# Making a row tile's scale on GpSimd instead of VectorE in a cumulative-difference matmul

## The chip, the core and the metric

One core of a Trainium2 chip runs the whole kernel. Its engines are TensorE (PE in the profile; its weight loads are PEld), VectorE (DVE), ScalarE (ACT), GpSimd (POOL) and SyncE (SP), which issues the DMAs. The metric is the device time of one execution in microseconds (us). The kernel before took 1449.84 us, the median of 3 runs (1449.72 to 1450.08).

## The reference

```python
def reference(x, w):                      # x: 8 x 2048 x 2048, w: 2048 x 2048, float32
    cs = np.cumsum(x, axis=1)
    diff = cs - np.concatenate([np.zeros(...), cs[:, :-1, :]], axis=1)
    return np.matmul(diff, w).astype(np.float32)
```

The difference of the cumulative sums is x itself up to rounding, so what is to be computed is x @ w: a 16384 x 2048 matrix times a 2048 x 2048 matrix.

## The kernel before

**Tiles.** x is cut into 128 row tiles of 128 rows. The first four (rows 0 to 3 in the code's counting of tiles) are multiplied in bf16 in a plain way while the weights are still being loaded. The other 124, tiles 4 to 127, go in groups of four through a Strassen-like scheme of fewer products on float16 blocks of W (`B11` to `B22`, and their differences `T1` to `T4`), with sums of row tiles made on VectorE. Products collect in PSUM; ACT copies them out with a scale (`keep`, line 636), VectorE adds further ones (`add`, line 639), and stores go out on SP's queue.

**Scales.** Row tiles and weights are brought into the range of float16 first. For W, ACT sums up absolute values (`measure`, line 273), VectorE takes the maximum (`greatest_of_w`, line 288), GpSimd makes an all-reduce over the partitions out of it (line 289), once for each half of W's columns, and VectorE makes the reciprocal (`scale_of_w`, lines 293 and 294), with which W's blocks are scaled (`block`, lines 342 and 346).

For each of the 124 row tiles the steps are:

1. `load` (line 113): two DMAs on SP's queue bring the 128 x 2048 tile into one of a few places in `F`.
2. `weigh` (line 125): ACT sums the absolute values of each half into a column of the small tile `of`; two operations of 128 x 1024.
3. `scale_of` (lines 142 and 144): VectorE adds the two sums, with a floor (`m`), and takes the reciprocal (`s`), both 128 x 1.
4. `unit_of` (line 150): GpSimd multiplies `uw`, the scale of W's two halves, by `m`. The result is the factor of `keep` and `add`.
5. `narrow` (line 164): ACT writes the tile in float16, multiplied by `s`; two operations.
6. `turn` (line 177): two transposing DMAs on SP's queue bring the float16 tile into the layout of TensorE's stationary operand (`x`).

**Order.** Each engine works through its own queue in order. The helper `after` chains the operations of one engine in the order in which the program asks for them. The start-up (lines 184 to 514), a first group (`group_plain`) and a second one (`group_half`) are written out by hand; all further groups follow the list `ORDER`, in which each step has its place (`scale.h`, `unit.h`, `narrow0.h` and so on). In the start-up the scale of tile 4 is asked for while the right half of W is still being brought in, before its maximum is known; the units and the scales of tiles 6 and 5 come behind that maximum. The first group uses tiles 4, 6, 5 and 7 in this order: its third product reads tile 6, its fifth a sum made out of tile 5.

**GpSimd's queue before.** Besides four memsets it holds a change of its configuration (MODIFY_POOL_CONFIG), the two all-reduces, another change of configuration, and the 124 operations of `unit_of`.

Of the kernel before, what the change touches and what calls it, by code (L numbers as in the profile page):

```python
# [10 lines left out]
def kernel(  # L11
# [6 lines left out]
    nc = tc.nc  # L18
    P = 128
# [10 lines left out]
    f32 = mybir.dt.float32  # L30
    ADD = mybir.AluOpType.add
    SUB = mybir.AluOpType.subtract
    MUL = mybir.AluOpType.mult
    MAX = mybir.AluOpType.max
# [5 lines left out]
    TINY = 1e-34  # L40
# [11 lines left out]
    const = ctx.enter_context(tc.tile_pool(name="const", bufs=1))  # L52
# [19 lines left out]
    uw = const.tile([P, 2], f32, name="uw")  # L72
    uinv = const.tile([P, 2], f32, name="uinv")

    waste = const.tile([P, NH], mybir.dt.uint8, name="waste")
    F = const.tile([P, 5, NH], f32, name="F")
    turned_x = [
# [10 lines left out]
    def after(engine, ask):  # L88
        if engine in last:
            with tc.issue_after(last[engine].ins):  # L90
                said = ask()
        else:
            said = ask()
        last[engine] = said[-1] if isinstance(said, tuple) else said
        return said
# [38 lines left out]
    def scale_of(t):  # L134
        if t < END:
            m2 = sums_of.pop(t)
            m, s = (m2[:, i : i + 1] for i in (2, 3))
            u = m2[:, 4:6]
            scales[t], unit[t] = s, u
            after(  # L140
                "dve",
                lambda: nc.vector.tensor_scalar(m, m2[:, :1], m2[:, 1:2], TINY, ADD, MAX),  # L142
            )
            after("dve", lambda: nc.vector.reciprocal(s, m))  # L144
            sizes[t] = m

    def unit_of(t):
# [38 lines left out]
    with ExitStack() as head:  # L186
# [229 lines left out]
        def bring(ko):  # L416
            fetch(1, ko)
            cast(1, ko)
            measure(1, ko)
            if ko == AHEAD:  # L420
                scale_of_w(0)
            if ko > AHEAD:
                turn_left(1)
            if ko == 10:
                load(PLAIN, 0)
                load(PLAIN, 1)
                weigh(PLAIN)
                scale_of(PLAIN)
            if ko == 11:
                narrow(PLAIN)  # L430
# [51 lines left out]
        for k in range(KH):  # L482
            block(B12, 0, 1, k, "dve")
            if k == 1:
                scale_of(PLAIN + 2)
            if k % 2:
                if k // 2:
                    finish_row(k // 2)
# [12 lines left out]
        turn(PLAIN + 2)  # L501
        weigh(PLAIN + 1)
        scale_of(PLAIN + 1)
        unit_of(PLAIN + 1)
        narrow(PLAIN + 1)
# [830 lines left out]
```

## Time and profile before

| what | value |
|---|---|
| time, median of 3 runs | 1449.84 us |
| span of the profiled execution, first to last instruction | 1447.4 us |
| TensorE busy | 1437.9 us (99%) |
| VectorE busy | 1319.0 us (91%) |
| ACT busy | 970.5 us (67%) |
| GpSimd busy | 43.8 us (3%) |
| TensorE in the chain that ended last | 97% |

The profile gives the span of the one profiled execution and no separate time for it beyond that; the runs are timed apart from it. A row of the timeline begins with the start in us from the span's start and the busy time in us, then the engine, the line, the operation, output and inputs, shapes, and how many operations the row merges; the idle time of the engine just before it and the event that seems to have ended it stand in brackets. A row of the view by line gives lowest, median and highest duration in ns, then the first and the last start in us. A row of the table by stretches gives the stretch, its length, and the busy times of PE, PEld, DVE, ACT and POOL, the granted TensorE clock, the DMA share and GB/s. POOLq is GpSimd's queue, SPq that of SyncE.

### The profile page before, as it was taken

To read this page: it belongs to the slowest core of one execution; us is meant where nothing else is said; L and a number is where in the kernel's file an instruction comes from. 1 tells how busy PE (TensorE), PEld (TensorE's weight loads), DVE (VectorE), ACT (ScalarE), POOL (GpSimd) and SP (SyncE) were. 2 spreads that over 40 slices of the span, in tenths; PEclk is the share of its full clock that TensorE was granted. 3 is DMA by queue.
4 is the path that set the end of the run, shared out by engine and by line. 5 is a ranking of instruction groups with operands and counts; after the bars stand their busy time and mean duration, and the time that the engine had idled before them with its cause. 6 is when DMAs were issued, how large, how long until landed. Compare 5 with 4: busy or idle time off the path is not lost.

```text
span 1447.4 us, 20191 instructions
## 1 busy us (share of the span) xinstructions
PE 1437.9 (99%) x6686; PEld 651.6 (45%) x6692; DVE 1319.0 (91%) x2310; ACT 970.5 (67%) x1472; POOL 43.8 (3%) x130
## 2 busy tenths in 40 slices
PE   8999999999999999999999999999999999999998
PEld 4444444444444444444444444444444444444443
DVE  4899899999999999999999999999999999999998
ACT  6987566666666776666666667666667766666662
POOL 0011000000000000000000000000000000000000
PEclk9999999999999999999999999999999999999999
DMA  9999788899888898888899888998878998889973
GB/s 363 368 257 298 200 234 232 239 253 253 226 224 239 238 254 245 231 233 236 248 247 232 234 238 233 262 240 234 228 234 240 252 234 239 226 242 248 255 200 127
DMA packets 378199, 351.58 MB, mean 243 GB/s; under 512 B 274800, under 2 KB 274800, under 8 KB 377968
## 3 DMA queue, kind: packets, MB, share of 16 engines
q1 hardware_dynamic: 378096, 350.31, 86.5%
q8 instruction: 52, 0.85, 0.2%
q14 instruction: 51, 0.42, 0.1%
HBM read 150.99 MB, written 134.22 MB: 197 GB/s over the span
## 4 chain that ended last, share of the span: by engine, by line
PE 97%; DMA 2%; DVE 0%; SPq 0%; issue 0%; DVEq 0%
PE b L628 62%; PE b L609 33%; PE b L304 2%; DMA W<-in_w_dram 2%; DMA W<-in_x_dram 0%; DVE c L639 0%; PE b L464 0%; SPq L225 0%; DVE wb L267 0%; SPq L259 0%; DVEq L267 0%; DVEq L639 0%
## 5 line engine op out<-in xcount | busy, mean ns | idle before, releaser
L639 DVE SCALAR_TENSOR_TENSOR c<-b,of,c 128x512 f32<-128x512 f32 x790 | 573.6, 746 | 71.1 <-PE b L628 61.4
L609 PE MATMUL b<-W,x 128*128 128x512 f16 x2144 | 507.1, 379 | 0.0
L636 ACT ACTIVATE c<-b,of 128x512 f32<-128x512 f32 x492 | 312.7, 680 | 220.2 <-PE b L628 113.8
L628 PE MATMUL b<-W,x 128*128 128x512 f16 x1904 | 454.9, 379 | 0.0
L164 ACT ACTIVATE F<-F,of 128x1024 f16<-128x1024 f32 x246 | 282.3, 1148 | 175.6 <-DVE of L144 173.4
L628 PEld LDWEIGHTS <-x 128*128 128x128 f16 x2500 | 244.6, 98 | 295.4 <-issue 1.0
L609 PEld LDWEIGHTS <-x 128*128 128x128 f16 x2144 | 209.7, 98 | 253.3 <-issue 0.5
L125 ACT ACTIVATE waste<-F 128x1024 uint8<-128x1024 f32 x246 | 259.3, 1054 | 8.3 <-DMA F<-in_x_dram 6.2
L628 PEld LDWEIGHTS <-inner 128*128 128x128 f16 x1644 | 160.8, 98 | 194.0
L628 PE MATMUL b<-W,inner 128*128 128x512 f16 x940 | 241.2, 379 | 0.0
L599 DVE TENSOR_TENSOR x<-x,x 128x1024 f16<-128x1024 f16 (+1 forms) x390 | 227.1, 583 | 3.3
L628 PE MATMUL b<-flow,x 128*128 128x512 f16 x584 | 149.9, 379 | 0.0
L628 PE MATMUL b<-inner 128*128 128x512 f16 x472 | 121.1, 379 | 0.0
L955 DVE TENSOR_TENSOR flow<-W 128x2048 f16<-128x2048 f16 x87 | 105.7, 1215 | 0.0
L1053 DVE TENSOR_TENSOR b<-b,c 128x512 f32<-128x512 f32 x116 | 80.4, 693 | 12.7 <-PE b L628 12.7
L150 POOL TENSOR_SCALAR of<-uw,of 128x2 f32<-128x2 f32 x124 | 42.6, 357 | 1299.6 <-DVE of L142 717.1
L955 DVE TENSOR_TENSOR flow<-W,inner 128x2048 f16<-128x2048 f16 x58 | 70.7, 1220 | 0.0
L1046 ACT COPY c<-b 128x512 f32<-128x512 f32 x58 | 33.4, 576 | 51.2 <-PE b L628 51.2
L304 PE MATMUL b<-wb,xP 128*128 128x512 bf16 x234 | 53.2, 379 | 2.2 <-ACT wb L265 1.1
L599 DVE TENSOR_TENSOR inner<-x 128x512 f16<-128x512 f16 x117 | 49.3, 421 | 3.1 <-DMA x<-F 1.0
L1046 ACT COPY b<-b 128x512 f32<-128x512 f32 x87 | 51.2, 589 | 0.2 <-PE b L628 0.2
L599 DVE TENSOR_TENSOR inner<-x,inner 128x512 f16<-128x512 f16 x117 | 49.2, 421 | 2.0
(68 smaller groups left out, 517.5 us busy)
## 6 DMA issues: line engine op xcount, KB each, us to landing
F<-in_x_dram SPq DMA_DIRECT2D x246, 512.0 KB, 5.2
out_dram<-c SPq DMA_DIRECT2D x492, 256.0 KB, 3.0
W<-in_w_dram SPq DMA_DIRECT2D x32, 512.0 KB, 8.4
W<-in_x_dram SPq DMA_DIRECT2D x16, 256.0 KB, 7.8
x<-F SPq DMA_TRANSPOSE x246, 3.4
out_dram<-o SPq DMA_DIRECT2D x5, 256.0 KB, 7.0
out_dram<-wb SPq DMA_DIRECT2D x5, 256.0 KB, 7.0
xP<-in_x_dram SPq DMA_DIRECT2D x1, 1024.0 KB, 6.4
```

Of the source, the lines that this page charges most:

```text
L125: lambda: nc.scalar.activation(waste, where[t][i], ABS, scale=1.0 / ROW, accum_out=sums_of[t][:, i : i + 1],),
L150: after("pool", lambda: nc.gpsimd.tensor_scalar(u, uw, m, None, MUL))
L164: lambda: nc.scalar.activation(narrowed(t)[:, ds(i * NH, NH)], where[t][i], COPY, scale=s),
L304: lambda: nc.tensor.matmul(ps[r][n], xP[:, r, ko, :], wb[h, ko][:, ds(n * NB, NB)], start=(ko == 0), stop=(ko == KO - 1),),
L599: after("dve", lambda: nc.vector.tensor_tensor(dst.all, p.all, q.all, op))
L609: said = nc.tensor.matmul(to[n], a[k], b[k][:, n, :], start=(first and k == 0), stop=(k == KH - 1), skip_group_check=True,)
L628: said = nc.tensor.matmul(to, a[k], b[k], start=(first and k == 0), stop=(k == 3), skip_group_check=True)
L636: after("act", lambda: nc.scalar.activation(c, p, COPY, scale=u))
L639: after("dve", lambda: nc.vector.scalar_tensor_tensor(c, p, u, c, MUL, ADD))
L955: after("dve", lambda: nc.vector.tensor_tensor(in_twos(to), x, y, op))
L1046: after("act", lambda: nc.scalar.copy(c, p))
L1053: after("dve", lambda: nc.vector.tensor_tensor(t, p, s, ADD))
```

## The change

The two small operations of `scale_of` are asked of GpSimd. The second is no reciprocal there but a power: the tensor `m` raised, element by element, to a constant tensor `minus` that holds -1, which VectorE writes once at the start of the program.

```diff
     uinv = const.tile([P, 2], f32, name="uinv")
 
+    minus = const.tile([P, 1], f32, name="minus")
+    nc.vector.memset(minus, -1.0)
     waste = const.tile([P, NH], mybir.dt.uint8, name="waste")
...
             after(
-                "dve",
-                lambda: nc.vector.tensor_scalar(m, m2[:, :1], m2[:, 1:2], TINY, ADD, MAX),
+                "pool",
+                lambda: nc.gpsimd.tensor_scalar(m, m2[:, :1], m2[:, 1:2], TINY, ADD, MAX),
             )
-            after("dve", lambda: nc.vector.reciprocal(s, m))
+            after(
+                "pool",
+                lambda: nc.gpsimd.tensor_tensor(s, m, minus, mybir.AluOpType.pow),
+            )
             sizes[t] = m
```

In the changed kernel the sum stands in line 144, the power in line 148, `unit_of` in line 155, `narrow` in line 169 and the all-reduce in line 294.

## The prediction

> **What bounds the kernel now.** I read the page first, then the busy times of stretches of the span.
>
> ```profile
> span 1447.4 us, 20191 instructions
> PE 1437.9 (99%) x6686; PEld 651.6 (45%) x6692; DVE 1319.0 (91%) x2310; ACT 970.5 (67%) x1472; POOL 43.8 (3%) x130
> ...
> PE 97%; DMA 2%; DVE 0%; SPq 0%; issue 0%; DVEq 0%
> ```
>
> ```profile
> 0.00:34.00 34.00, 29.16 (x166) 13.59 (x170) 16.84 (x29) 22.10 (x33) 0.19 (x4) 1.00 0.95 360
> 34.00:92.00 58.00, 57.84 (x266) 26.15 (x269) 49.88 (x90) 54.33 (x85) 6.02 (x6) 1.00 1.05 342
> ...
> 186.00:1419.00 1233.00, 1233.00 (x5713) 558.91 (x5712) 1142.88 (x2016) 826.12 (x1256) 30.50 (x112) 1.00 0.87 237
> ```
>
> The columns after the length are the busy times of PE, PEld, DVE, ACT and POOL, then the granted clock. From 186 to 1419 us TensorE is busy for 1233.00 of 1233.00 us at clock 1.00. So work taken off VectorE buys nothing there: TensorE cannot start earlier what it already does without a gap. A change can move the end only by opening a gap on TensorE. I therefore look for the place where TensorE's next operand hangs on a row tile's scale with little to spare. That is the start-up, 34 to 92 us, where ACT too is nearly full (54.33 of 58.00). A gap opened there stays, since nothing later is idle enough to give it back.
>
> **What the change removes.**
>
> ```profile
> L142 DVE TENSOR_SCALAR of<-of x124: 202/205/214, 56.5 to 1406.4; 128x1 f32<-128x1 f32 x124
> ...
> L144 DVE RECIPROCAL of<-of x124: 162/164/166, 56.8 to 1406.7; 128x1 f32<-128x1 f32 x124
> ```
>
> VectorE loses 124 x (0.205 + 0.164) = 45.8 us. In the full stretch TensorE hides all of it: worth 0. ACT's waits for the scale shorten or lengthen with the new chain, also hidden in the middle of the kernel, as one row tile there shows:
>
> ```profile
> 653.70 0.19 ACT L125 ACTIVATION_READ_ACCUMULATOR waste<-F 128x1 f32 x1
> ...
> 657.93 0.20 DVE L142 TENSOR_SCALAR of<-of 128x1 f32<-128x1 f32 x1
> ...
> 658.37 2.33 ACT L164 ACTIVATE F<-F,of 128x1024 f16<-128x1024 f32 x2 [0.80 <-DVE of L144]
> ```
>
> The sums were ready at 653.89 and VectorE's queue came to them 4.0 us later. A GpSimd pair of up to about 4 us loses nothing there. The memset of -1 on VectorE stands first in its queue; the idle time that follows there hides it, and at most it costs the length of the memset now first.
>
> ```profile
> 0.84 0.27 DVE L207 MEMSET F<- 128x256 uint32 x1 [0.84 <-PEq L1320]
> ...
> 5.17 0.69 DVE L235 CAST W<-W 128x1024 bf16<-128x1024 f32 x1 [1.91 <-DMA W<-in_x_dram]
> ```
>
> **What it adds on GpSimd.** Two operations of one element per partition, the second waiting on the first. Nearest rows:
>
> ```profile
> L150 POOL TENSOR_SCALAR of<-uw,of x124: 287/287/1900, 75.2 to 1407.1; 128x2 f32<-128x2 f32 x124
> ...
> 41.22 0.70 POOL L289 PARTITION_ALL_REDUCE uw<-wtop  x1 [40.79 <-DVE wtop L288]
> 64.76 0.35 POOL L289 PARTITION_ALL_REDUCE uw<-wtop  x1 [22.84 <-DVE wtop L288]
> 75.21 3.60 POOL L150 TENSOR_SCALAR of<-uw,of 128x2 f32<-128x2 f32 x3 [10.09 <-DVE of L144]
> ```
>
> A small GpSimd operation takes 0.287 us, or 3.60 / 3 = 1.2 us among VectorE's adds at 75 us, at most 1.9. No row shows a power. Call the pair p: from 2 x 0.287 = 0.6 us to 2 x 1.2 = 2.4, or 3.8 by the longest. I take p = 1.4, the middle of 0.6 and 2.4, since VectorE is dense in the start-up. Call the single `unit` operation 0.8, between 0.29 and 1.2.
>
> **What it moves: GpSimd's code library.** This decides the forecast. The all-reduce over partitions lives in another library than the ordinary operations, and the build puts a reload wherever the queue passes from one to the other. Before, the queue is: reload, all-reduce of W's left half, all-reduce of the right half, reload, then only ordinary operations. After, the pair of row 4 falls between the two all-reduces, so the order is: reload, all-reduce, **reload**, pair of row 4, **reload**, all-reduce, reload, `unit` of row 4, pair of row 6, `unit` of row 6, pair of row 5 and so on. Two reloads are added and all stand in order. What one costs:
>
> ```profile
> L289 POOLq MODIFY_POOL_CONFIG  x2: 11/11/11, 1.0 to 1.0; - x2
> ...
> L150 POOLq MODIFY_POOL_CONFIG  x2: 83/83/83, 65.1 to 65.1; - x2
> ```
>
> ```profile
> 64.49 0.17 DVE L288 TENSOR_REDUCE wtop<-wsum 128x1 f32<-128x16 f32 x1 [1.24 <-ACT waste L273]
> 65.15 0.15 DVE L293 TENSOR_SCALAR uw<-uw 128x1 f32<-128x1 f32 x1 [0.49 <-POOL uw L289]
> ```
>
> The second reload is issued at 65.1, just behind the all-reduce (64.76 + 0.35). The next GpSimd operation, `unit` of row 4, needs only `uw`, done at 65.30, and the scale of row 4, done at 57; yet it starts at 75.21, with the two for rows 6 and 5 right behind it. So a reload holds the queue for X = 75.2 - 65.1 = 10 us; the page's "DVE of L144" beside it is only the last event before. In the old kernel nobody needed GpSimd in that time. For the library of the all-reduce the trace gives only bounds: 0, and the 40 us from 1.0 to 41.22. I take the same 10, the one reload that shows its length.
>
> The Trainium skill ("GPSIMD Engine Reference", 2.1 Instruction dispatch) gives about 6 us (5.95) for the first call after such a load. The row here disagrees for the ordinary library: 10 us. By that figure for every reload the sum below would be an estimated 5 us, not 12.
>
> **The start-up, step by step.** Rows needed:
>
> ```profile
> 56.29 0.19 ACT L125 ACTIVATION_READ_ACCUMULATOR waste<-F 128x1 f32 x1
> 57.56 2.31 ACT L164 ACTIVATE F<-F,of 128x1024 f16<-128x1024 f32 x2
> 68.62 2.36 ACT L164 ACTIVATE F<-F,of 128x1024 f16<-128x1024 f32 x2
> 71.65 1.06 ACT L125 ACTIVATE waste<-xP 128x1024 uint8<-128x1024 f32 x1 [0.67 <-DMA xP<-in_x_dram]
> ...
> 72.83 1.06 ACT L125 ACTIVATE waste<-xP 128x1024 uint8<-128x1024 f32 x1
> ...
> 75.17 2.33 ACT L164 ACTIVATE xP<-xP,of 128x1024 f16<-128x1024 f32 x2 [1.19 <-DVE of L144]
> ...
> 87.61 2.33 ACT L164 ACTIVATE F<-F,of 128x1024 f16<-128x1024 f32 x2 [0.48 <-DVE of L144]
> 89.85 2.40 ACT L636 ACTIVATE inner<-b,of 128x512 f32<-128x512 f32 x4
> ```
>
> ```profile
> 71.09 14.09 PE L609 MATMUL b<-W,x 128*128 128x512 f16 x64
> 85.01 3.62 PE L609 MATMUL b<-W,S 128*128 128x512 f16 x16
> 88.46 4.86 PE L609 MATMUL b<-W,x 128*128 128x512 f16 x21
> ```
>
> ```profile
> x<-F SPq DMA_TRANSPOSE x246, 3.4
> ```
>
> The `narrow` steps of rows 4, 6, 5 and 7 are the four L164 rows. (1) The reload behind the first all-reduce (from 41.9) ends at 51.9, before row 4's sums at 56.48: hidden, 4.6 us to spare. (2) Pair of row 4: 56.5 + 1.4 = 57.9; ACT starts row 4 0.3 late, which moves the maximum of W from 64.66 to about 65. (3) Reload until 67.9, all-reduce until 68.25: 3.1 us later than 65.11; VectorE waits there, with the rest of W's blocks behind it. (4) Reload until 78.25, `unit` of row 4 until 79.05, pair of row 6 until 80.45. Row 6 is narrowed from 80.45 instead of 68.62; ACT and, behind it, the transposes on SP's queue, the load of row 7 and the stores all wait. (5) ACT then needs 2.36 for row 6 and two sum steps of 72.83 - 71.65 = 1.18 for row 5, so row 5's pair begins at 80.45 + 4.7 = 85.15 and row 5 is narrowed from 86.55 instead of 75.17: 11.4 late. (6) ACT's next 12 us run as before, then row 7's pair takes 1.4 where the wait was 0.48: row 7 is 12.3 late. (7) The four copies to `inner` behind it empty PSUM; the third of them ended at 89.85 + 3 x 0.6 = 91.65, and TensorE wanted that bank at 88.46 + 3.45 = 91.9. No slack to speak of, so TensorE is about 12.3 late from there on.
>
> The gap opens earlier: the third product of the first group reads row 6 transposed at 71.09 + 2 x 3.45 = 78.0, and now has it at about 80.45 + 1.2 + 3.4 = 85. So I expect 7 us of idle TensorE there and the other 5 between there and 105 us.
>
> In one formula, as long as W's maximum is there first: row 6's pair ends at E = 56.5 + p + X + 0.35 + X + 0.8 + p; the delay is (E + 4.7 + p - 75.17) + (p - 0.48) = E + 2p - 70.95, so **2X + 4p - 13.3**. With X = 10 and p = 1.4 it is 12.3 us. Later row tiles wait on nothing but p, with the slack shown at 653.
>
> **Sum.** The profiled span of 1447.4 is 2.4 below the median of 1449.84, launch and end lying around it; a delay inside adds to both: 1449.84 + 12.3 = 1462.
>
> **Rivals.**
> *The all-reduce's library is quick to load* (under 7 us): the second added reload hides behind the wait for W's maximum; all-reduce ends near 65.2, row 6's pair at 65.2 + 10 + 0.8 + 1.4 = 77.4; delay 77.4 - 70.95 + 2.8 = 9.3: **1459**. Nothing in the trace speaks against it but the length of the other one.
> *The 10 us are only half load*, the rest something that overlaps here: X = 5, all-reduce at its old time, delay 65.2 + 5 + 2.2 - 70.95 + 2.8 = 4.3: **1454**. Against it: nothing else in the row fills the time. The Trainium skill's 5.95 ("GPSIMD Engine Reference", 2.1 Instruction dispatch) lies near this case, an estimated 1455.
> *The power is slow*: p = 5 gives 2 x 10 + 20 - 13.3 = 27, **1477**; it begins to cost in the full stretch only beyond the 4 us shown there. No row speaks for or against it.
>
> ```profile
> 75.05 4.88 DVE L513 TENSOR_TENSOR W<-W 128x1024 f16<-128x1024 f16 x8
> ...
> 87.49 3.68 DVE L591 TENSOR_TENSOR W<-W 128x1024 f16<-128x1024 f16 x6
> ```
>
> *GpSimd holds VectorE up.* In the full stretch VectorE has 1233.00 - 1142.88 = 90 us idle and sheds 112 x 0.369 = 41: 131 us for 112 pairs, 1.17 each. If each pair stopped it for all of 1.4 us, 26 us more would come to the 12: **1488**. Against it: VectorE's adds took 4.88 / 8 = 0.61 us beside three GpSimd operations and 3.68 / 6 = 0.61 beside one. The Trainium skill ("SBUF — State Buffer", Who interferes with whom) says that a VectorE operation with two SBUF inputs and a GpSimd operation that reads SBUF lock each other out for a whole instruction, whichever came first; the trace shows GpSimd waiting (1.2 for 0.287 us), not VectorE.
>
> *Not slower*: the gap from 65.1 to 75.2 belongs to something else and a reload is short. Row 6's pair is done at 65.2 + X + 2.2; with no more than X = 0.75 no delay is left, and TensorE's full stretch makes it **1449.8**. For it: the releaser named by the page. Against it: three operations queued up and ran together at 75.21.
> *Faster* needs TensorE idle time that VectorE causes; from 34 to 92 it has 0.16 us.
>
> **How the numbers follow.** The forecast reaches from 1459 (p = 0.6: 20 + 2.4 - 13.3 = 9.1) to 1466 (p = 2.4: 16.3), and to 1469 if the first reload, among the full load queues, overruns its 4.6 us of cover by 3: chance 0.60. Quick all-reduce library 0.15, half load 0.05, slow power 0.09, VectorE held up 0.03, not slower 0.08. A difference under 0.2% (2.9 us) cannot be told from none here. The range 1454 to 1473 leaves out not slower, VectorE held up and most of slow power, under 2 in 10. Of not slower, 0.06 is within 0.2% and 0.02 faster, so slower has 0.92.
>
> **What would show it.** Right: reloads at about 41.9, 58 and 68; the second all-reduce at about 68 and the first `unit` at about 78; row 6 narrowed from about 80; TensorE idle some 12 us between 70 and 105 and nowhere else. Wrong: the all-reduce still at 64.8 (quick library), the first `unit` straight behind it (no reload cost), L148 over 2 us (slow power), or gaps on TensorE after 186 us, which would mean that GpSimd disturbs VectorE.

## The result

The changed kernel took 1464.93 us, the median of 4 runs (1464.84 to 1465.48); the kernel before, beside it, took 1449.78 (1449.63 to 1450.08). The ratio is 1.0107, with a 95% interval of 1.0095 to 1.0118: 15.15 us slower. The forecast was 1462, with a range of 1454 to 1473.

The page of the changed kernel, with its span, busy times and the chain of work that ended last; then busy times by stretch (length, PE, PEld, DVE, ACT, POOL, granted clock, DMA share, GB/s):

```profile
span 1463.1 us, 20311 instructions
...
PE 1441.8 (99%) x6686; PEld 652.4 (45%) x6692; DVE 1289.6 (88%) x2063; ACT 967.4 (66%) x1472; POOL 261.4 (18%) x378
...
PE 94%; DMA 2%; issue 1%; DVE 1%; ACT 1%; POOL 1%; SPq 0%; DVEq 0%
```

```profile
0.00:34.00 34.00, 29.43 (x166) 13.61 (x170) 16.89 (x30) 22.10 (x33) 0.19 (x4) 1.00 0.95 359
34.00:92.00 58.00, 45.80 (x204) 20.20 (x207) 39.79 (x67) 41.29 (x68) 12.02 (x11) 0.93 0.78 267
201.00:1434.00 1233.00, 1233.00 (x5715) 558.96 (x5713) 1116.72 (x1794) 823.66 (x1256) 229.59 (x334) 1.00 0.87 237
```

The span grew by 15.7 us. TensorE's new idle time lies in one place: it was busy for 57.84 of the 58 us from 34 to 92 before and is busy for 45.80 now. The last row is the full stretch, moved by 15 us: TensorE is again busy for 1233.00 of 1233.00 us at clock 1.00. VectorE was relieved of 26 us there (1142.88 to 1116.72), and that bought nothing. Over the whole span its busy time fell by 29.4 us (1319.0 to 1289.6) and not by the 45.8 that the forecast added up; since TensorE hides it, this changes nothing.

GpSimd's queue tells why. First its changes of configuration by line (lowest, median and highest ns, then first and last start), then its timeline:

```profile
L144 POOLq MODIFY_POOL_CONFIG  x2: 82/82/83, 41.9 to 41.9; - x2
...
L294 POOLq MODIFY_POOL_CONFIG  x4: 6/8/11, 1.0 to 59.0; - x4
...
L155 POOLq MODIFY_POOL_CONFIG  x2: 83/83/83, 66.6 to 66.7; - x2
```

```profile
41.23 0.70 POOL L294 PARTITION_ALL_REDUCE uw<-wtop  x1 [40.81 <-DVE wtop L293]
56.59 1.14 POOL L144 TENSOR_SCALAR of<-of 128x1 f32<-128x1 f32 x1 [14.65 <-ACT waste L127]
57.82 1.19 POOL L148 TENSOR_TENSOR of<-of,minus 128x1 f32<-128x1 f32 x1
66.29 0.38 POOL L294 PARTITION_ALL_REDUCE uw<-wtop  x1 [7.28 <-DVE wtop L293]
76.45 5.79 POOL L155 TENSOR_SCALAR of<-uw,of 128x2 f32<-128x2 f32 x1 [9.78 <-DVE wb L339]
81.62 1.35 POOL L144 TENSOR_SCALAR of<-of 128x1 f32<-128x1 f32 x1
83.06 0.60 POOL L148 TENSOR_TENSOR of<-of,minus 128x1 f32<-128x1 f32 x1
```

The reloads stand at 41.9, 59.0 and 66.7. The last holds the queue for 9.78 us; then one operation that takes 0.29 us elsewhere runs for 5.79; and only then, from 81.6 to 83.7, comes the pair for row 6. Beside that long operation VectorE has eight adds back to back, from 75.98 to 80.87:

```profile
75.98 4.89 DVE L518 TENSOR_TENSOR W<-W 128x1024 f16<-128x1024 f16 x8
```

The four `narrow` steps on ACT (line 169) and the copies around them, then TensorE's timeline:

```profile
59.04 2.33 ACT L169 ACTIVATE F<-F,of 128x1024 f16<-128x1024 f32 x2 [1.38 <-POOL of L148]
...
83.69 2.33 ACT L169 ACTIVATE F<-F,of 128x1024 f16<-128x1024 f32 x2 [13.45 <-POOL of L148]
...
89.32 2.33 ACT L169 ACTIVATE xP<-xP,of 128x1024 f16<-128x1024 f32 x2 [1.09 <-POOL of L148]
91.56 0.67 ACT L478 ACTIVATE x<-b,uw 128x512 f32<-128x512 f32 x1
...
103.54 2.33 ACT L169 ACTIVATE F<-F,of 128x1024 f16<-128x1024 f32 x2 [2.15 <-POOL of L148]
105.77 2.40 ACT L641 ACTIVATE inner<-b,of 128x512 f32<-128x512 f32 x4
```

```profile
68.84 3.61 PE L469 MATMUL b<-W,xP 128*128 128x512 f16 x16 [1.02 <-ACT wb L337]
72.29 7.22 PE L614 MATMUL b<-W,x 128*128 128x512 f16 x32
88.12 1.46 PE L614 MATMUL b<-W,x 128*128 128x512 f16 x3 [8.60 <-DMA x<-F]
92.28 8.80 PE L614 MATMUL b<-W,x 128*128 128x512 f16 x29 [2.70 <-ACT x L478]
100.92 3.62 PE L614 MATMUL b<-W,S 128*128 128x512 f16 x16
```

Before, rows 6, 5 and 7 were narrowed from 68.62, 75.17 and 87.61; now from 83.69, 89.32 and 103.54. TensorE's fifth product (the one on `S`) began at 85.01 and now begins at 100.92, 15.9 us later. The three waits on TensorE add up to 1.0 + 8.6 + 2.7 = 12.3 us. Most of the rest of the 15.9 is matmuls that ran slower: 29 of them in 8.80 us and 3 in 1.46, where 64 had taken 14.09, so 32 would take 7.05, and these took 3.2 more. In the table by short stretches the granted clock (third number from the end) is seen to fall and come back:

```profile
82.00:84.00 2.00, 0.00 (x0) 0.00 (x0) 0.86 (x2) 0.31 (x1) 1.88 (x4) 0.87 0.00 0
84.00:86.00 2.00, 0.00 (x0) 0.00 (x0) 0.00 (x0) 1.97 (x3) 0.00 (x0) 0.50 0.00 0
...
94.00:96.00 2.00, 2.00 (x6) 0.70 (x5) 0.00 (x0) 2.00 (x4) 0.00 (x0) 0.50 0.88 223
96.00:98.00 2.00, 2.00 (x8) 0.85 (x7) 1.99 (x3) 2.00 (x3) 0.00 (x0) 0.72 0.83 188
98.00:100.00 2.00, 2.00 (x11) 0.88 (x9) 1.93 (x5) 1.72 (x3) 0.00 (x0) 1.00 0.99 384
```

TensorE stops at 72.29 + 7.22 = 79.5. The mean of 0.87 from 82 to 84 is that of a fall to 0.50 at about 83.5, some 4 us later.

### The profile page after: what moved, and what is told of

The parts are those of the page before. It is cut to its first block, busy times and chain, and to the rows that moved or that the text cites. A ratio compares the mean times of both kernels' runs of the same rounds, so it can differ in the third digit from the quotient of the medians.

```text
span 1463.1 us, 20311 instructions
## 1 busy us (share of the span) xinstructions
PE 1441.8 (99%) x6686; PEld 652.4 (45%) x6692; DVE 1289.6 (88%) x2063; ACT 967.4 (66%) x1472; POOL 261.4 (18%) x378
## 4 chain that ended last, share of the span: by engine, by line
PE 94%; DMA 2%; issue 1%; DVE 1%; ACT 1%; POOL 1%; SPq 0%; DVEq 0%
PE b L633 61%; PE b L614 32%; DMA W<-in_w_dram 2%; DVE W L347 0%; DMA W<-in_x_dram 0%; POOL of L155 0%; ACT waste L278 0%; PE b L309 0%; DVE c L644 0%; ACT F L169 0%; ACT waste L127 0%; POOL of L148 0%; ACT xP L169 0%; POOL of L144 0%; SPq L230 0%
## 5 line engine op out<-in xcount | busy, mean ns | idle before, releaser
L641 ACT ACTIVATE c<-b,of 128x512 f32<-128x512 f32 x492 | 316.1, 681 | 326.9 <-PE b L633 179.0
L614 PE MATMUL b<-W,x 128*128 128x512 f16 x2144 | 510.6, 381 | 11.3 <-DMA x<-F 8.6
L144 POOL TENSOR_SCALAR of<-of 128x1 f32<-128x1 f32 x124 | 120.1, 969 | 1091.3 <-ACT waste L127 1091.3
L148 POOL TENSOR_TENSOR of<-of,minus 128x1 f32<-128x1 f32 x124 | 80.2, 647 | 10.3
L155 POOL TENSOR_SCALAR of<-uw,of 128x2 f32<-128x2 f32 x124 | 61.1, 503 | 9.8 <-DVE wb L339 9.8
```

Of the source, the lines that this page charges most:

```text
L144: lambda: nc.gpsimd.tensor_scalar(m, m2[:, :1], m2[:, 1:2], TINY, ADD, MAX),
L148: lambda: nc.gpsimd.tensor_tensor(s, m, minus, mybir.AluOpType.pow),
L155: after("pool", lambda: nc.gpsimd.tensor_scalar(u, uw, m, None, MUL))
L614: said = nc.tensor.matmul(to[n], a[k], b[k][:, n, :], start=(first and k == 0), stop=(k == KH - 1), skip_group_check=True,)
L641: after("act", lambda: nc.scalar.activation(c, p, COPY, scale=u))
```

## The experiments

The theory: the loss comes from the reload that now stands ahead of row 6's scale, and from the pairs of operations in the start-up, lengthened by VectorE's adds. The rivals: the two added reloads cost time of their own; the power is slow; GpSimd disturbs VectorE all through the kernel; the fallen clock makes part of the loss; the first operation behind a reload is long by itself. Each ratio below is against the kernel before, run beside it (medians 1449.40 to 1449.63). Row 4, 6, 5 or 7 stands for the row tile of that number, and its pair for the sum and the power of its scale.

### Rows 4, 6 and 5 back on VectorE

```diff
+            if t > PLAIN + 2:
                 after("pool", lambda: nc.gpsimd.tensor_scalar(m, ...))
                 after("pool", lambda: nc.gpsimd.tensor_tensor(s, m, minus, ...pow))
+            else:
+                after("dve", lambda: nc.vector.tensor_scalar(m, ...))
+                after("dve", lambda: nc.vector.reciprocal(s, m))
```

> The pairs of rows 4, 6 and 5 stay on VectorE, the other 121 are on GpSimd as in the changed kernel; GpSimd's queue has no added reload. Theory A (all of the loss is in the start-up, behind the reloads): 1449.8 us, within 1 of the kernel before, TensorE without a gap after 34 us. Rival B (the pairs on GpSimd also cost something in the 1233 us in which TensorE is full, by holding VectorE up or by making ACT late): a part of the 15 us stays, 1452 or more, with gaps on TensorE after 186 us.

Measured: 1450.90 us (1450.54 to 1451.14), ratio 1.0009 (0.9999 to 1.0018). With 121 of the 124 pairs still on GpSimd nearly the whole loss is gone. The expectation of no gap after 34 us, within 1 us of the kernel before, was missed by a little. From its timelines and its table by stretches:

```profile
87.51 1.11 POOL L145 TENSOR_SCALAR of<-of 128x1 f32<-128x1 f32 x1 [10.91 <-ACT waste L127]
```

```profile
93.71 0.38 PE L621 MATMUL b<-W,x 128*128 128x512 f16 x1 [1.44 <-ACT inner L648]
```

```profile
186.00:1419.00 1233.00, 1233.00 (x5715) 559.01 (x5713) 1117.07 (x1794) 824.22 (x1256) 230.62 (x336) 1.00 0.87 237
```

The loss belongs to the first three scales, and not to the power as such or to GpSimd beside VectorE in the full stretch. What is left, 1.3 us, is small (the interval of the ratio just reaches 1), but the trace shows where it lies: row 7's pair takes 2.0 us, and TensorE waits 1.44 + 0.20 for the copies to `inner` behind it, as the forecast's step 7 said ("No slack to speak of").

### Row 4 alone on GpSimd, and rows 6 and 5 alone

The condition above becomes `t == PLAIN`, and then `t in (PLAIN + 1, PLAIN + 2)`. All other rows are on VectorE.

> Only the pair of row 4 is on GpSimd, which is what adds the two reloads; all other pairs are on VectorE. Theory A (row 6's pair stands behind reload and unit; the second added reload is hidden): ACT narrows row 4 1.4 us late, W's maximum and the second all-reduce are 1.5 us late, the unit of row 4 comes at about 76.5 and nobody waits for it: 1 to 2 us lost, 1451 to 1452. Rival C (each reload costs its 10 us): 10 us or more, 1460.

> Only the pairs of rows 6 and 5 are on GpSimd, no reload is added: the one reload behind the second all-reduce is there as in the kernel before. Theory A: row 6 waits from 65.1 for the end of that reload at 75.2, then for the unit of row 4 and its pair, so it is narrowed at 78 to 82 and nearly all of the loss is back: 1460 to 1464. Rival C (the two added reloads are the loss): about 1450.

Measured: row 4 alone 1450.77 us (1450.44 to 1451.13), ratio 1.0008 (0.9999 to 1.0017); rows 6 and 5 alone 1459.89 us (1457.83 to 1463.66), ratio 1.0079 (1.0062 to 1.0096). GpSimd with row 4 alone, which holds both added reloads:

```profile
66.38 0.38 POOL L301 PARTITION_ALL_REDUCE uw<-wtop  x1 [7.28 <-DVE wtop L300]
76.56 2.69 POOL L162 TENSOR_SCALAR of<-uw,of 128x2 f32<-128x2 f32 x3 [9.80 <-DVE wb L346]
```

So with row 4 alone the added reloads cost about 1 us together, that of a maximum of W which comes later. What costs is a reload which had been there before. It was harmless as long as only `unit_of` waited behind it, and with rows 6 and 5 alone, when no reload is added, 10.3 us are lost in the median. These four runs lie 5.8 us apart, and the profiled one is the fastest, with 8.2 us lost. In it the reload held the queue for 7.0 us and not 9.8:

```profile
72.11 0.30 POOL L162 TENSOR_SCALAR of<-uw,of 128x2 f32<-128x2 f32 x1 [6.98 <-DVE W L354]
...
78.64 2.06 POOL L145 TENSOR_SCALAR of<-of 128x1 f32<-128x1 f32 x1 [4.54 <-ACT waste L127]
```

So row 6 was narrowed at 74.00, 5.4 us later than before, and not at 78 to 82 as expected. Row 5's pair, which began 0.7 us before the end of VectorE's eight adds, took 3.1 us, and row 5 was narrowed at 81.80, 6.6 us later than before. TensorE's longest wait was 5.5 us, for ACT's copy of a leftover product (the line that is L478 in the changed kernel), which is queued behind row 5's `narrow`.

### VectorE's eight adds held until row 6's scale is there

```diff
+    held = const.tile([P, 1], f32, name="held")
...
+        after("dve", lambda: nc.vector.tensor_copy(held, scales[PLAIN + 2]))
         # then the adds of T1, line 518
```

> The changed kernel, but VectorE reads row 6's scale before its eight adds of T1, so that no add runs while GpSimd makes the unit of row 4 (5.79 us in the changed kernel) and the pair of row 6. Theory D (VectorE's two-input adds keep GpSimd out): the unit takes 0.3 us, row 6 is narrowed at about 78 instead of 83.7, and 4 to 6 us come back: 1459 to 1461. Rival E (the first operation after the reload is long by itself, as code is still being fetched): the unit stays above 5 us and the time at 1465.

Measured: 1461.49 us (1460.54 to 1462.54), ratio 1.0081 (1.0066 to 1.0096), 11.9 us lost in place of 15.15. GpSimd and ACT:

```profile
78.21 0.30 POOL L156 TENSOR_SCALAR of<-uw,of 128x2 f32<-128x2 f32 x1 [11.32 <-issue]
...
84.18 1.71 POOL L145 TENSOR_SCALAR of<-of 128x1 f32<-128x1 f32 x1 [4.37 <-ACT waste L128]
```

```profile
79.53 2.33 ACT L170 ACTIVATE F<-F,of 128x1024 f16<-128x1024 f32 x2 [9.07 <-POOL of L149]
```

The `unit` operation takes 0.30 us in place of 5.79 although a reload stands just ahead of it: it was the adds that kept it, and not the reload's aftermath. The time is 0.5 us above the expected 1459 to 1461. The gain of 3.3 is smaller than the 5.5 saved there, since the reload took 11.3 here and the first operation of row 5's pair now runs beside the last of the adds (1.71 + 0.97).

### No reload, and then no reload with the adds held too

GpSimd copies each partition's own maximum of W here, so the maximum over the partitions is left out and the library needn't change between the two halves of W. One change of configuration is left, at 41.8, and nobody waits behind it.

```diff
-            nc.gpsimd.partition_all_reduce(u, m, P, bass_isa.ReduceOp.max)
+            after("pool", lambda: nc.gpsimd.tensor_copy(u, m))
```

and in the second kernel also

```diff
+        after("dve", lambda: nc.vector.tensor_copy(held, scales[PLAIN + 1]))
         # then the adds of T1
```

> The changed kernel with the two all-reduces over the partitions left out: GpSimd copies each partition's own maximum of W instead, so that the output is another one and the library never changes between the two halves (one reload stays, behind the first copy, with some 14 us to spare). All 124 pairs are on GpSimd. Theory A (reloads ahead of row 6 are the loss, not the pairs): row 6 narrowed before 71, 1450 to 1453 us. Rival B (the pairs on GpSimd themselves are the loss): above 1458.

> The kernel without the all-reduces over the partitions (1458.5 us; GpSimd copies each partition's own maximum of W instead, so its output is another one), and VectorE reads row 5's scale before its eight adds of T1, so that no add runs beside row 5's pair, whose first operation took 6.12 us there. Theory (two causes and no third: the reload ahead of row 6, and VectorE's run of two-input adds that keeps GpSimd out): that operation takes 0.3 to 0.5 us, row 5 is narrowed at about 77 instead of 83, and the time is 1450.5 to 1453. Rival (something else holds the pairs of the start-up up): it stays above 1456.

Measured: no reload 1458.49 us (1458.24 to 1458.95), ratio 1.0063 (1.0046 to 1.0080); with the adds held behind row 5's scale too 1452.49 us (1451.94 to 1454.24), ratio 1.0023 (1.0012 to 1.0034). GpSimd without the reload, VectorE beside it, and GpSimd when the adds are held as well:

```profile
68.37 1.72 POOL L144 TENSOR_SCALAR of<-of 128x1 f32<-128x1 f32 x1 [0.89 <-ACT waste L127]
...
75.82 6.12 POOL L144 TENSOR_SCALAR of<-of 128x1 f32<-128x1 f32 x1 [4.39 <-ACT waste L127]
```

```profile
75.67 4.89 DVE L518 TENSOR_TENSOR W<-W 128x1024 f16<-128x1024 f16 x8
```

```profile
76.25 0.31 POOL L145 TENSOR_SCALAR of<-of 128x1 f32<-128x1 f32 x1 [4.38 <-ACT waste L128]
```

In the first kernel the time that was expected without the reload (1450 to 1453) didn't come; it is the rival's, above 1458. Row 6 was nearly in time again (its pair from 68.4, narrowed at 71.17 for 68.62), and still 9.1 us were lost. Now it was row 5's pair that began 0.15 us behind the start of the eight adds, and its first operation took 6.12 us. With both removed, 3.0 us are left, and TensorE's waits of 2.1 for `inner` (behind row 7's pair) and 1.0 for the first products account for them. The time of the second kernel is within the expected 1450.5 to 1453. So there are two causes, and each covers part of the other: taking away the reload alone gives 6.1 of the 15.15 us back, holding the adds alone 3.3, both together 12.1.

### Row 7 on VectorE too

The condition becomes `t > PLAIN + 3`, so that rows 4 to 7 are scaled by VectorE.

> As the kernel with the pairs of rows 4, 6 and 5 on VectorE, which was at 1450.9, but row 7's too. Theory H (what was left there is row 7's pair, 2.0 us among VectorE's adds instead of 0.48, ahead of the copies into inner that TensorE waits for): that wait of 1.6 us is gone and the time is that of the kernel before, 1449.4 to 1450.0. Rival B (a cost of the other 120 pairs): stays at 1450.9.

Measured: 1455.14 us (1454.66 to 1455.41), ratio 1.0040 (1.0025 to 1.0055): 5.7 us lost, against 1.3 with row 7 on GpSimd, which neither expectation had. Row 7's wait is gone, and what comes behind it is 2.0 us earlier. So the second pair behind it, which began at 107.99 in the other kernel, begins at 105.99 here and falls into VectorE's next run of eight adds. GpSimd, VectorE and TensorE:

```profile
105.99 3.38 POOL L145 TENSOR_SCALAR of<-of 128x1 f32<-128x1 f32 x1 [7.12 <-ACT waste L127]
...
115.56 1.23 POOL L145 TENSOR_SCALAR of<-of 128x1 f32<-128x1 f32 x1 [3.68 <-ACT waste L127]
```

```profile
103.17 4.89 DVE L603 TENSOR_TENSOR W<-W 128x1024 f16<-128x1024 f16 x8
107.98 1.22 DVE L608 TENSOR_TENSOR inner<-W 128x2048 f16<-128x2048 f16 x1
```

```profile
123.51 0.38 PE L621 MATMUL b<-W,x 128*128 128x512 f16 x1 [3.65 <-ACT c L648]
```

The early pair is done no sooner than the late one: `narrow` starts at 110.92 here and at 110.71 there. The next pair begins at 115.56 beside two more adds with two inputs and takes 2.7 us, where it took 0.9 there; its `narrow` starts at 118.34 for 116.35, and the copies behind it on ACT at 122.79 for 120.81. TensorE is 2.0 us early and the copies are 2.0 us late, which makes its wait of 3.65 + 0.20. Behind the wait the granted clock is 0.53 from 124 to 126 us and 0.62 from 126 to 128, an estimated 1.7 us more. With an earlier start the kernel is slower. That the adds did it is read from the trace; no further run tests it.

### The gap filled

36 matmuls into banks that are free, on data that is there, are put ahead of the product that reads row 6:

```diff
+        for i in range(36):
+            after("pe", lambda: nc.tensor.matmul(Z[i % 2], B11[0][:, 0, :P], ...))
         product(Y, A11h, B11, True)
```

> The changed kernel with 36 matmuls of 128x512 that nobody reads (about 7.8 us) ahead of the third product of the first group, in the gap in which TensorE waits for row 6 and after which its granted clock was 0.50 for some 10 us. Theory F (the slow matmuls behind the gap cost their 3 us): the clock stays at 1.00 and the time falls to about 1462. Rival G (ACT's chain through row 7 to the copies into inner is the same length, so TensorE only waits later): the clock stays at 1.00 and the time at 1464 to 1465, with a new wait of TensorE for ACT's copies into inner.

Measured: 1465.35 us (1465.09 to 1466.40), ratio 1.0112 (1.0097 to 1.0127), no gain against the changed kernel. The matmuls filled 7.93 us, and a wait of 5.00 for the leftover's copy on ACT came behind them:

```profile
79.53 7.93 PE L714 MATMUL b<-W 128*128 128x512 f16 x36
...
92.46 8.97 PE L614 MATMUL b<-W,x 128*128 128x512 f16 x32 [5.00 <-ACT x L478]
```

In these 5 us the clock fell again, so neither expectation's clock of 1.00 came about and the run doesn't price the clock by itself. It shows that the end of the gap, 92.3 or 92.5, is set by row 5's `narrow` and the copy behind it, and not by row 6's transposes.

### The price of the power

One kernel has a product in place of the power (`pow` becomes `MUL`). Two have rows 4, 6 and 5 on VectorE and 6 or 16 further powers in each pair from row tile 12 on, written to a column that nobody reads.

> The changed kernel with the power replaced by a product of the same two operands; the row tiles are scaled by another number, so the output is another one. It prices the power itself: if the two-input form is what costs, the product takes the same 0.56 us undisturbed; if it is the power, 0.3 us. The time stays within 2 us of 1465 either way.

> As the kernel with the pairs of rows 4, 6 and 5 on VectorE, but from row 12 on each pair has six further powers in front of the one that counts, into an unused column: a pair of about 4.5 us. Theory (a row tile in the full stretch has some 4 us to spare, and TensorE alone sets the pace): within 2 us of 1450.9. Rival (GpSimd's work holds VectorE up, or ACT is near its limit): more than 5 us slower, with gaps on TensorE after 186 us.

> As with six further powers from row 12 on, but sixteen: a pair of about 10 us, far over the 4 us that a row tile has to spare. Expected: ACT waits some 5 us and more for each row's scale, TensorE gets gaps after 186 us, and the time is over 1500 us.

Measured, one run each for the product and for 16 powers: 1463.62 and 2450.91 us; with 16 powers ACT waited 1126.9 us in all for scales. With 6 powers 1619.97 us (1617.87 to 1622.89), ratio 1.1179 (1.1162 to 1.1195). The line of the power in the changed kernel and in that with the product:

```profile
L148 POOL TENSOR_TENSOR of<-of,minus x124: 559/612/1427, 57.8 to 1419.3; 128x1 f32<-128x1 f32 x124
```

```profile
L148 POOL TENSOR_TENSOR of<-of,minus x124: 189/232/1048, 58.0 to 1417.9; 128x1 f32<-128x1 f32 x124
```

The power costs 0.38 us more than a product. With the product 14.2 us are lost by this one run, in place of 15.15: the power's own price is a small part. With 6 more powers a pair becomes some 6.0 us long; the expected time, within 2 us of 1450.9, is missed by far, and the stretch that TensorE had filled shows gaps:

```profile
186.00:1419.00 1233.00, 1130.44 (x5032) 500.31 (x5031) 985.28 (x1577) 726.01 (x1112) 573.09 (x889) 0.97 0.75 210
```

The slack in the full stretch so ends somewhere between the pair of the changed kernel (0.97 + 0.65 = 1.6 us in the mean) and 6 us. That a pair of 4 us would be free, as the forecast read out of one row tile at 653 us, was not shown. It isn't refuted either: over the kernel with rows 4, 6 and 5 on VectorE (1450.9) the two kernels lose 169 and 1000 us on 116 row tiles, with pairs of some 6.0 and 12.7 us, and a straight line through these two points reaches no loss at a pair of about 4.6 us, an estimate.

## Why the prediction was right, and where it was off

**The bound and the place: right.** TensorE's full stretch kept its 1233.00 of 1233.00 us, VectorE's relief was worth nothing, and the gap opened at the third product of the first group.

**Step 1, the first added reload hidden: right.** Row 4's pair began at 56.59, when the sums were there. **Step 2, row 4:** its pair took 2.4 us, not 1.4, and ACT started row 4 at 59.04, not 57.9.

**Step 3, the second added reload: wrong.** The all-reduce was put at 67.9, behind a reload of 10 us. It ran at 66.29, 0.14 behind the maximum on VectorE (65.98 + 0.17), 7.3 us after the change at 59.0. So this reload takes 7.3 us or less here and hides behind the wait for the maximum, which is the mechanism of the rival "The all-reduce's library is quick to load"; its 1459 did not come out, because of the next step.

**Step 4, the third reload: right in length** (9.8 for 10). **The `unit` operation was the mis-sized term:** 0.8 us in the sum, 5.79 in the trace, 5.17 of them before the pair could start. The quoted row of three operations in 3.60 us, beside the same eight adds in the kernel before, was taken for the price of company with VectorE. It isn't one: the same adds let these three through at 1.2 each, and kept a single one out until just after their end in the changed kernel, in that without a reload, in the filled one and in that with the product. The Trainium skill ("SBUF — State Buffer", Who interferes with whom) was cited for a lock that lasts a whole instruction. The trace bears out that VectorE wins (its adds took 0.61 us as before), but the wait here lasted over the rest of a run of eight instructions, and the measurement decides.

**Steps 5 to 7.** With the measured terms the formula's own sum comes out. Row 6's pair was done at 83.66 for 80.45: the all-reduce 1.6 earlier, the reload 0.2 shorter, `unit` 4.4 longer, the pair 0.6 longer, + 3.2. Row 5's pair took 1.0 for 1.4 and row 7's 2.06 for 1.4, together + 0.3. So 12.3 + 3.5 = 15.8, against 15.9 measured at row 7 and 15.15 in the time. The forecast of 12 us of idle TensorE came out at 12.3, but that is luck, as it is made of other parts: 1.0 ahead of line 469, 8.6 (for 7) at row 6, then 2.7 for the copy of line 478, which the forecast didn't name as queued behind row 5. It left out altogether the slower matmuls at a clock of 0.50. Luck is also in the total: the 1.6 us by which the all-reduce came earlier made up for part of the 4.4 that the `unit` operation was longer. The copies to `inner` were 15.9 us late as well (105.77 for 89.85), so a clock at 1.00 need not have saved its 3.2 us; this stays open.

**The rivals.** Half load, X = 5: no, 9.8 us, and not under 7.0 in any run that has this reload. Slow power: it is dear (0.61 us), not slow enough to matter. GpSimd holding VectorE up: no; the adds and the other costly groups of VectorE kept their durations. Not slower: the gap before 75.21 was the reload, as the same wait for the same line stands in every run that has one, and the run without it has its first `unit` at once.

**The Trainium skill's 5.95 us** ("GPSIMD Engine Reference", 2.1 Instruction dispatch) for the first call after a load would have made 5 us out of 12. From the change of configuration behind the second all-reduce to the first ordinary operation the eleven kernels that have both show 7.0 to 11.3 us, the kernel before 10.1 and the changed one 9.8: the measurement decides.

## What to carry to other kernels

Before work goes to an engine that looks idle, go through its queue in order: a change of GpSimd's library that costs nothing while nobody waits behind it becomes 10 us on the path as soon as an urgent operation stands there, and here the pairs of three of the 124 row tiles made nearly the whole loss. A tiny GpSimd operation that somebody waits for is better not put beside a run of two-input VectorE adds: its price in such a place may be its price elsewhere several times over (0.3 against up to 6 us here). Relief for an engine is worth something only where it ends the wait of the one that bounds the kernel.

## What the runs showed that was not expected

- A GpSimd operation of 0.30 us took 4.98 (with the product), 5.32 (gap filled), 5.79 (changed kernel) and 6.12 us (no reload) when it began soon after the start of VectorE's eight adds, and 3.38 when it began in the second half of another eight. Held behind the scale, the same adds left it at 0.30. But a run of such adds doesn't always keep GpSimd out. In the kernel before, three operations got through the same adds in 3.60 us, and in the changed kernel row 7's pair began inside a run of seven adds and took 1.09 and 0.85 us (its rows and the adds' stand below). What decides between the two stays open, and it wasn't tried.
- The reload's length varies with the kernel, from 7.0 to 11.3 us. What sets it wasn't tried either; one trace per kernel doesn't show whether it also varies from run to run.
- The granted clock fell to 0.50 some 4 us after TensorE stopped (79.5 to about 83.5), and came back to 1.00 only about 5 us after it had started again at 92.3. The Trainium skill ("TensorE: Matmul & The Clock Gate", Part 1) has half the clock after an idle window of about 3.4 us. The trace agrees in the half, and its 4 us is near. In the filled kernel, though, the clock fell about 2 us after the matmuls had ended (87.5 to about 89.5, by a mean of 0.88 from 88 to 90), so the delay isn't one fixed figure here.
- Taking a wait away can cost more than the wait: with row 7's scale back on VectorE 5.7 us were lost in place of 1.3, as later scales met VectorE's adds.

The seven adds of the changed kernel, and row 7's pair inside them:

```profile
99.39 4.29 DVE L596 TENSOR_TENSOR W<-W 128x1024 f16<-128x1024 f16 x7
```

```profile
101.48 1.09 POOL L144 TENSOR_SCALAR of<-of 128x1 f32<-128x1 f32 x1 [11.89 <-ACT waste L127]
102.65 0.85 POOL L148 TENSOR_TENSOR of<-of,minus 128x1 f32<-128x1 f32 x1
```
